# Two weight units staged in device memory, and another order of norms and transposes at two changes of stage

## Chip, cores, metric

One core of a Trainium2 chip runs the whole program; the other cores are idle. The metric is the device time of one execution in microseconds (us). Three executions of the kernel before took 946.19, 947.06 and 951.06 us, median 947.06.

## What is computed

The reference is a decoder trunk of two layers on 512 tokens of 1024 channels, all in float32. Layer 0 mixes tokens by trailing means over 2, 4, 8 and 16 tokens; layer 1 is attention over a window of 128 keys, with 16 query heads, 4 shared key and value heads and a sink logit per head. Each layer ends with a gated feed-forward part of width 2816 with a causal convolution of width 3. Every part has a norm ahead of it and one behind it:

```
for layer in range(2):
    h = rms_norm(x, mix_pre_g[layer])
    if layer == 0: m = pool_mixer(h, pool_w, pool_scale)
    else:          k, v = rms_norm(x, kv_norm_g) @ w_kv ; q = rope(h @ w_q)
                   m = attention(q, rope(k), v, sinks) @ w_o
    x = x + rms_norm(m, mix_post_g[layer])
    f = conv_glu_ffn(rms_norm(x, ffn_pre_g[layer]), w_in, conv_w, conv_b, w_out)
    x = x + rms_norm(f, ffn_post_g[layer])
```

## The kernel before

**Tiling.** The tokens are four blocks of 128 (b = 0 to 3), the channels eight chunks of 128. Every float32 product is made of three matmuls on reduced-precision parts: each operand is split into a high part (a copy that rounds, on ScalarE, `wh`, `xTh`, `gh`) and a low part (the difference, on VectorE, `wl`, `xTl`, `gl`), and `mm3` adds high x high, high x low and low x high in PSUM.

**Weights.** All large weights come as 95 numbered units of 128x2048, in the order of use. 1 to 22 are layer 0's up projection, 23 to 42 its down projection, 43 and 44 K and V, 45 to 48 Q, 49 to 52 the output projection, 53 to 74 layer 1's up projection, 75 to 94 its down projection. `load` brings a unit to a `raw` buffer (two of them) on SP's DMA queue, `split` makes its high and low part in one of three slots (two kinds of unit have a place of their own), and `ahead` splits three units ahead of use. Units 43 to 46 are made otherwise: `prepare` loads them half by half during layer 0's up projection, multiplies a norm's gain into them, splits them, and stores both parts in device memory (`ready`); later `split` only loads the finished parts into a slot, by DMAs that ScalarE issues. The first two units of an up projection, 53 and 54 in layer 1, are split in quarters by `low`, the low part on GpSimd.

**Order.** The order of the instructions on TensorE, VectorE, ScalarE and GpSimd is the order in which the code is written; each engine works through its own list and waits for others by semaphores. The order on SP's queue is set by the scheduler.

**Layer 0's second pass** (`pass2`). The down projection is done by a scheme with seven products on 2x2 blocks; the second pass has the last three. While TensorE goes through the pairs p = 0 to 10 for the products 3 and 2, the other engines prepare coming units (`soon(k)`: one unit's split, then the split of the matching G tile), and finish blocks 2 and 3 of the stream, which need only earlier products: `update(b)` adds to x, `pre_a(b)` takes the squares on ScalarE (`rstd_of`) and the inverse root on GpSimd in three 128x1 steps (an addition of epsilon, an addition of the two halves, a power), `pre_b(b)` scales x by it, `to_attention(b)` transposes the result on TensorE (tiles `tr_a`, L299) into `xTh_a` and `xTl_a`. Before, blocks 2's and 3's `pre_a` and `pre_b` stand together behind p = 1, and `to_attention` behind p = 5 and p = 6. In units: p = 4 and 5 need unit 39, p = 6 and 7 unit 40, p = 8 and 9 unit 41, p = 10 unit 42. The last three pairs are taken for block 0 and 2 first (i = 0), then for 1 and 3. Behind this pass come the K and V projections of blocks 2 and 3 (`kp`, `vp`), then `to_attention(0)`. `pass2` serves both layers; the calls under `then` are made in layer 0 only.

**End of attention.** The output projection is added up in all eight PSUM banks (`op`), first the products of one pair of heads, then those of the other. Block by block, `o_proj(1, b)` ends it with 24 matmuls; `post_norm` adds the normed result to x (squares on ScalarE, L247; root on GpSimd, L254 to L258; gain, L272, and update, L274, on VectorE), `pre_norm` makes the feed-forward part's input from it (the same squares and root, then L291), and `transpose_in` transposes it on TensorE (`tr_f`) and splits it (ScalarE L302, VectorE L303). Between these stand the quarters of units 53 and 54 (casts L189 on ScalarE, subtractions L193 on GpSimd). Then `start1` begins the up projection (`u`) with the units 53 and 54 on blocks 0 and 1; block 2's transposes follow behind the first of them.

Of the kernel before, what the change touches and what calls it, by code (L numbers as in the profile page):

```python
# [39 lines left out]
N_UNITS = 95  # L40
N_SLOTS = 3
# [29 lines left out]
def build(nc, tc, ctx, a, out):  # L71
# [44 lines left out]

    mhalf = pc.tile([P, 1], F32, tag="mhalf", name="mhalf")
# [11 lines left out]
    ready = {i: [dram(f"{n}{i}", 2048) for n in ("hi", "lo")] for i in (U_K, U_V, U_Q, U_Q + 1)}  # L129
# [29 lines left out]
    def prepare(i, h):  # L159
# [5 lines left out]
        for k in range(4):  # L165
# [77 lines left out]
    def rstd_of(src, junk, name):  # L243

        ss = pc.tile([P, 4], F32, tag="ss", name=f"ss_{name}", bufs=6)
        for h in range(2):
            nc.scalar.activation(junk[h], src[h], AF.Square, scale=1.0 / math.sqrt(D),  # L247
                                 accum_out=ss[:, h : h + 1])
            if h == 0:
                add_eps(ss, 0)  # L250
        return rstd_end(ss)

    def add_eps(ss, h):
        nc.gpsimd.tensor_scalar(ss[:, h : h + 1], ss[:, h : h + 1], EPS, None, ALU.add)  # L254

    def rstd_end(ss):
        nc.gpsimd.tensor_tensor(ss[:, 2:3], ss[:, 0:1], ss[:, 1:2], ALU.add)
        nc.gpsimd.tensor_tensor(ss[:, 3:4], ss[:, 2:3], mhalf, ALU.pow)  # L258
        return ss[:, 3:4]

# [21 lines left out]
    def pre_b(b):  # L282
        for h in range(2):
            nc.scalar.activation(halves(xna[b])[h], halves(x[b])[h], AF.Identity, scale=xnr[b])
# [230 lines left out]
    def first(l, xT, accs, p1, G2):  # L515
# [54 lines left out]
        for j in range(NF):  # L570
# [7 lines left out]
            if l == 0 and 3 <= j < 11:  # L578
                prepare((U_K, U_V, U_Q, U_Q + 1)[(j - 3) // 2], (j - 3) % 2)
# [32 lines left out]
    def pass2(l, p2, G2, X, post_row):  # L612
# [52 lines left out]
        def square(z, i, q):  # L665

            b, h = i + (2 if z[0] == "2" else 0), int(z[1]) - 1
            first = b not in ss
            if first:
                ss[b] = pc.tile([P, 4], F32, tag="ss", name=f"ss_p_f{l}{b}", bufs=6)  # L670
            nc.scalar.activation(X[q][i], Z[z][i], AF.Square, scale=1.0 / math.sqrt(D), accum_out=ss[b][:, h : h + 1])  # L671
            if first:
                add_eps(ss[b], h)
# [20 lines left out]
        for m in range(3):  # L694
# [3 lines left out]
            if m < 2:  # L698
                nc.vector.tensor_tensor(Z["22"][m], Z["12"][m], X[7][m], ALU.add)
                add("21", m, 7)  # L700
                square("22", m, 7)
# [11 lines left out]
        for p in range(NP - NT):  # L713
            for q in of:
                make(q, p, (0, 1))
            if p == 0:
                for i in range(2):
                    add("21", i, 4)
                    square("21", i, 4)
                    root(2 + i)  # L720
                soon(5)
                for i in range(2):
                    gain("21", i)
                for i in range(2):
                    update(2 + i)
                soon(6)
            if p == 1:
                then(pre_a, 2)
                then(pre_a, 3)
                soon(7)  # L730
                then(pre_b, 2)
                then(pre_b, 3)
            if p == 5:
                then(to_attention, 2)
# [415 lines left out]
```

## Time and profile before

| | |
|---|---|
| median of three executions | 947.06 us |
| the profiled execution's own time | 945.61 us |
| its span, first to last instruction | 943.5 us |
| busy on TensorE / VectorE / ScalarE / GpSimd | 97% / 69% / 50% / 36% |
| mean granted TensorE clock | 0.988 |

A row of a timeline gives start and duration in us, engine, source line, operation, the tiles written and read, their shape, how many like instructions in a row are merged, and in brackets the idle time of the engine just before with what ended it. PE is TensorE, PEld its weight loads, DVE VectorE, ACT ScalarE, POOL GpSimd, SP the engine that issues most DMAs. Matmuls overlap, so their durations are longer than their distance. A row of the view by stretches gives the stretch, its length, busy us of each engine with the number of instructions, the granted clock, the DMA engines' busy share and GB/s. A row of DMA issues gives the number, the size of one, and the median us from issue to landing. Tile names in the profile lack their numbers: `wl` is the low part of any unit.

### The profile page before, as it was taken

Reading aid. Unit: us, or ns where it says so; the run is one execution under the profiler, and the core shown is the slowest. Engines: PE = TensorE matmul, PEld = TensorE weight load, DVE = VectorE, ACT = ScalarE, POOL = GpSimd, SP = SyncE. Lnnn points to the kernel's source line nnn. Section 1 sums busy time; section 2 is a strip of 40 time slices with the busy share of each in tenths; the row PEclk is TensorE's granted clock in tenths of the full one; section 3 lists DMA queues with packets and bytes.
Section 4 is the critical chain, followed back from the end, with each engine's and each line's share of the span. In section 5 each row is a group of like instructions: output and inputs, shape, how many; then the busy total and the mean of one; then the engine's idle time right before and its main releaser. Section 6 shows DMA issues by size and latency. Waiting matters only on the chain.

```text
span 943.5 us, 12767 instructions
## 1 busy us (share of the span) xinstructions
PE 911.8 (97%) x4702; PEld 781.1 (83%) x4702; DVE 654.3 (69%) x940; ACT 469.5 (50%) x823; POOL 337.9 (36%) x389
## 2 busy tenths in 40 slices
PE   9999999999999999899999996999999999999996
PEld 8888888888888877799899885988888888888784
DVE  5878888765567788545999747466555565677886
ACT  5645444533345566454788634433333433455562
POOL 3725444433341002325566226144444433410001
PEclk9999999999999999899999997999999999999998
DMA  8356899855555664740112214444555555456652
GB/s 304 123 192 222 324 332 319 296 198 189 190 177 149 217 211 147 278 162 19 45 46 91 90 45 149 142 179 179 187 206 198 197 204 191 160 164 196 222 186 87
DMA packets 43024, 170.10 MB, mean 180 GB/s; under 512 B 5073, under 2 KB 6609, under 8 KB 34898
## 3 DMA queue, kind: packets, MB, share of 16 engines
q1 hardware_dynamic: 41810, 160.90, 48.7%
q10 hardware_dynamic: 1152, 8.39, 2.3%
q8 instruction: 37, 0.61, 0.3%
q14 instruction: 25, 0.20, 0.1%
HBM read 135.72 MB, written 33.55 MB: 179 GB/s over the span
## 4 chain that ended last, share of the span: by engine, by line
PE 76%; DVE 11%; DMA 3%; issue 3%; ACT 3%; POOL 3%; SPq 0%; POOLq 0%; DVEq 0%; ACTq 0%
PE u L307 17%; PE u L308 17%; PE u L306 17%; PE dn L306 4%; PE dn L307 4%; PE dn L308 4%; DVE xn_f L291 2%; DVE wl L227 2%; DVE P L895 1%; DMA raw<-in_ws_dram 1%; DVE x L274 1%; DMA raw<-t 1%; PE op L306 1%; PE op L307 1%; PE op L308 1%
## 5 line engine op out<-in xcount | busy, mean ns | idle before, releaser
L306 PE MATMUL u<-xTh_f,wh 128*128 128x512 f32 (+1 forms) x768 | 286.7, 373 | 4.5 <-ACT xTh_f L302 4.5
L307 PE MATMUL u<-xTl_f,wh 128*128 128x512 f32 (+1 forms) x768 | 286.2, 373 | 4.3 <-DVE xTl_f L303 4.3
L308 PE MATMUL u<-xTh_f,wl 128*128 128x512 f32 (+1 forms) x768 | 286.0, 372 | 0.0
L227 DVE TENSOR_TENSOR wl<-raw,wh 128x1024 fp32r<-128x1024 f32 (+1 forms) x158 | 204.6, 1335 | 14.2 <-ACT wh L226 13.9
L306 PEld LDWEIGHTS u<-xTh_f,wh 128*128 128x128 f32 x768 | 145.6, 190 | 30.1 <-ACT xTh_f L302 5.0
L307 PEld LDWEIGHTS u<-xTl_f,wh 128*128 128x128 f32 x768 | 145.5, 189 | 29.4 <-DVE xTl_f L303 4.8
L524 DVE SCALAR_TENSOR_TENSOR t<-u,conv,t 128x511 f32<-128x511 f32 x88 | 65.8, 748 | 148.0 <-ACT t L523 148.0
L308 PEld LDWEIGHTS u<-xTh_f,wl 128*128 128x128 f32 x768 | 145.5, 189 | 24.9
L226 ACT CAST wh<-raw 128x1024 fp32r<-128x1024 f32 (+1 forms) x158 | 156.8, 1041 | 12.7 <-DMA raw<-t 6.9
L523 ACT ACTIVATE t<-u,conv 128x512 f32<-128x512 f32 x88 | 68.2, 777 | 137.9 <-PE u L308 100.8
L544 POOL TENSOR_TENSOR G<-G,G 128x256 f32<-128x256 f32 x22 | 33.3, 1515 | 278.1 <-DVE G L539 278.1
L307 PE MATMUL dn<-wl,gh 128*128 128x512 f32 x276 | 108.1, 392 | 1.4 <-DVE wl L227 1.4
L308 PE MATMUL dn<-wh,gl 128*128 128x512 f32 x276 | 108.0, 391 | 1.2 <-DVE gl L637 1.2
L306 PE MATMUL dn<-wh,gh 128*128 128x512 f32 x276 | 108.1, 392 | 0.0
L532 ACT ACTIVATE t<-t 128x512 f32<-128x512 f32 x44 | 27.8, 632 | 104.6 <-DVE t L525 104.6
L525 DVE SCALAR_TENSOR_TENSOR t<-u,conv,t 128x510 f32<-128x510 f32 x88 | 65.9, 749 | 3.1
L307 PEld LDWEIGHTS dn<-wl,gh 128*128 128x128 f32 x276 | 52.1, 189 | 13.0 <-DVE wl L227 2.3
L254 POOL TENSOR_SCALAR ss_p_f<-ss_p_f 128x1 f32<-128x1 f32 x8 | 2.8, 354 | 166.6 <-ACT dn L671 166.6
L308 PEld LDWEIGHTS dn<-wh,gl 128*128 128x128 f32 x276 | 52.1, 189 | 12.4 <-DVE gl L637 1.6
L306 PEld LDWEIGHTS dn<-wh,gh 128*128 128x128 f32 x276 | 52.2, 189 | 10.8
L565 ACT CAST gh<-G 128x1024 fp32r<-128x1024 f32 x22 | 23.1, 1052 | 55.3 <-DVE G L563 40.8
L566 DVE TENSOR_TENSOR gl<-G,gh 128x1024 fp32r<-128x1024 f32 x22 | 28.0, 1274 | 26.6 <-ACT gh L565 21.1
(194 smaller groups left out, 1555.0 us busy)
## 6 DMA issues: line engine op xcount, KB each, us to landing
raw<-in_ws_dram SPq DMA_DIRECT2D x51, 1024.0 KB, 4.9
q<-in_ws_dram SPq DMA_DIRECT2D x44, 512.0 KB, 5.8
raw<-t SPq DMA_DIRECT2D x24, 768.0 KB, 5.5
t<-q SPq DMA_DIRECT2D x44, 256.0 KB, 2.9
t<-q SPq DMA_DIRECT2D x22, 512.0 KB, 2.7
raw<-in_ws_dram SPq DMA_DIRECT2D x22, 512.0 KB, 4.4
raw<-in_ws_dram SPq DMA_DIRECT2D x22, 256.0 KB, 3.9
r<-in_ws_dram SPq DMA_DIRECT2D x8, 512.0 KB, 7.0
```

The source lines that it names most:

```text
L226: nc.scalar.copy(hi[:, s], r[:, s])
L227: nc.vector.tensor_tensor(lo[:, s], r[:, s], hi[:, s].bitcast(F32), ALU.subtract)
L306: nc.tensor.matmul(acc, ah, bh, start=first, stop=False)
L307: nc.tensor.matmul(acc, ah, bl, start=False, stop=False)
L308: nc.tensor.matmul(acc, al, bh, start=False, stop=last)
L523: nc.scalar.activation(t, u, AF.Identity, bias=conv_col(l, ch, 3), scale=conv_col(l, ch, 2))
L524: nc.vector.scalar_tensor_tensor(t[:, 1:], u[:, : S - 1], conv_col(l, ch, 1), t[:, 1:], ALU.mult, ALU.add)
L525: nc.vector.scalar_tensor_tensor(t[:, 2:], u[:, : S - 2], conv_col(l, ch, 0), t[:, 2:], ALU.mult, ALU.add)
L532: nc.scalar.activation(tg, tg, AF.Gelu_apprx_tanh)
L544: nc.gpsimd.tensor_tensor(s1, s1, G2[:, p, 2, :], ALU.add)
L565: nc.scalar.copy(h, G1[:, o : o + 1024])
L566: nc.vector.tensor_tensor(lo, G1[:, o : o + 1024], h.bitcast(F32), ALU.subtract)
```

## The change

1. Units 53 and 54 join the units that `prepare` stages in device memory (`READY`). No gain belongs to them, so a half is one cast on ScalarE and one subtraction on VectorE. The twelve halves are no longer made in steps j = 3 to 10 of layer 0's up projection, one a step, but in two of every three steps from 3 to 19. At the end of attention eight ScalarE casts and eight GpSimd subtractions go, and four DMAs of 1 MB, issued by ScalarE, come: one pair ahead of block 0's `o_proj`, one ahead of block 1's. SP loads raw units 55 and 56 where 53 and 54 were loaded.
2. In `pass2`, in both layers, `soon(6)` goes ahead of the updates of blocks 2 and 3. In layer 0, `pre_a` and `pre_b` of block 2 come behind p = 2, then `soon(7)`, then block 3's; `pre_b` of these two blocks goes from ScalarE to VectorE; block 2's transposes go behind p = 7, block 3's behind the product 3 of the last three pairs for i = 0; V's loads go ahead of them, and block 1's last square and root ahead of block 0's norm.
3. At the end of attention `o_proj(1, 3)` is cut into its two halves, with block 1's transposes between them; block 0's transposes stand where they stood. On ScalarE and VectorE the split of the transposed block 0 now stands ahead of block 2's post-norm, that of block 1 ahead of block 3's; before, each stood between that block's post-norm and its pre-norm.
4. The instruction that preloads the Exp table reads `nsink` instead of a constant. The rest renames functions.

```
+READY = (U_K, U_V, U_Q, U_Q + 1, U_IN[1], U_IN[1] + 1)
...
-        for k in range(4):
+        if i >= U_IN[1]:
+            nc.scalar.copy(hi, r)
+            nc.vector.tensor_tensor(r.bitcast(F32R), r, hi.bitcast(F32), ALU.subtract)
+        for k in range(4 if i < U_IN[1] else 0):
...
     def pre_b(b):
         for h in range(2):
-            nc.scalar.activation(halves(xna[b])[h], halves(x[b])[h], AF.Identity, scale=xnr[b])
+            o, i = halves(xna[b])[h], halves(x[b])[h]
+            if b < 2:
+                nc.scalar.activation(o, i, AF.Identity, scale=xnr[b])
+            else:
+                nc.vector.tensor_scalar(o, i, xnr[b], None, ALU.mult)
...
-            if l == 0 and 3 <= j < 11:
-                prepare((U_K, U_V, U_Q, U_Q + 1)[(j - 3) // 2], (j - 3) % 2)
+            if l == 0 and j >= 3 and j % 3 != 2 and j < 21:
+                k = (j - 3) // 3 * 2 + j % 3
+                prepare(READY[k // 2], k % 2)
...
                 soon(5)
                 for i in range(2):
                     gain("21", i)
+                soon(6)
                 for i in range(2):
                     update(2 + i)
-                soon(6)
-            if p == 1:
+            if p == 2:
                 then(pre_a, 2)
+                then(pre_b, 2)
+                soon(7)
                 then(pre_a, 3)
-                soon(7)
-                then(pre_b, 2)
                 then(pre_b, 3)
             if p == 5:
-                then(to_attention, 2)
                 soon(8)
                 then(split, U_K)
-            if p == 6:
-                then(to_attention, 3)
+            if p == 7:
+                then(split, U_V)
+                then(to_attention, 2)
 
         for i in range(2):
             for q in of:
                 for p in range(NP - NT, NP):
                     make(q, p, (i,))
-        then(split, U_V)
+                if i == 0 and q == 3:
+                    then(to_attention, 3)
...
-        nc.scalar.activation(tab, mhalf, AF.Exp)
+        nc.scalar.activation(tab, nsink[:, 0:1], AF.Exp)
...
-        u0, u1 = U_IN[1], U_IN[1] + 1
         for b in range(NB):
-            u = (u0, u1)[b // 2]
-            o_proj(1, b, os[1, b])
+            if b < 2:
+                split(U_IN[1] + b)
+            o_proj(1, b, os[1, b], (0,))
+            if b == 3:
+                transpose_in(1, xnf[1], xT, "f1")
+            o_proj(1, b, os[1, b], (1,))
+            if b == 2:
+                transpose_in(0, xnf[0], xT, "f1")
             post_norm(b, acc[b], post_row, "m1", pa)
-            low(u, b % 2 * 2)
-            if b > 1:
-                transpose_in(b - 2, xnf[b - 2], xT, "f1")
             xnf[b] = pre_norm(b, pre_row, "f1")
-            low(u, b % 2 * 2 + 1)
```

The first place is VectorE's list in layer 0's second pass, before. Z2 is blocks 2 and 3 of the down projection; `wl40` is unit 40's low part, `gl3_0_3` that of the G tile used with it; `ss_n_a2` holds block 2's inverse root.

```order
L676 TENSOR_TENSOR Z2_0_2774<-Z2_0_2774,fpost0_724 128x512 x2
L685 SCALAR_TENSOR_TENSOR x2_75<-Z2_0_2774,ss_p_f02_2850,x2_75 128x512 x2
L685 SCALAR_TENSOR_TENSOR x3_76<-Z2_0_2774,ss_p_f03_2892,x3_76 128x512 x2
L227 TENSOR_TENSOR wl40_2968<-raw40_2919,wh40_2967 128x1024 x2
L637 TENSOR_TENSOR gl3_0_3_2976<-G2_0_729,gh3_0_3_2975 128x1024
L227 TENSOR_TENSOR wl41_3006<-raw41_2954,wh41_3005 128x1024 x2
L637 TENSOR_TENSOR gl3_0_4_3012<-G2_0_729,gh3_0_4_3011 128x1024
L303 TENSOR_TENSOR xTl_a_3068<-tr_a20_3069,xTh_a_3067 128x512
```

And the same piece in the changed kernel:

```order
L687 TENSOR_TENSOR Z2_0_2806<-Z2_0_2806,fpost0_728 128x512 x2
L232 TENSOR_TENSOR wl40_2996<-raw40_2951,wh40_2995 128x1024 x2
L650 TENSOR_TENSOR gl3_0_3_3004<-G2_0_733,gh3_0_3_3003 128x1024
L696 SCALAR_TENSOR_TENSOR x2_75<-Z2_0_2806,ss_p_f02_2882,x2_75 128x512 x2
L696 SCALAR_TENSOR_TENSOR x3_76<-Z2_0_2806,ss_p_f03_2924,x3_76 128x512 x2
L296 TENSOR_SCALAR xn_a2_3035<-x2_75,ss_n_a2_3036 128x512 x2
L232 TENSOR_TENSOR wl41_3045<-raw41_2986,wh41_3044 128x1024 x2
L650 TENSOR_TENSOR gl3_0_4_3051<-G2_0_733,gh3_0_4_3050 128x1024
L296 TENSOR_SCALAR xn_a3_3054<-x3_76,ss_n_a3_3055 128x512 x2
L232 TENSOR_TENSOR wl42_3100<-raw42_3001,wh42_3099 128x1024
L650 TENSOR_TENSOR gl3_0_5_3104<-G2_0_733,gh3_0_5_3103 128x512
```

Unit 40 with its G tile went ahead of the updates, and the two normalisations, each waiting for a root, now stand on VectorE between the units 40, 41 and 42.

The second place is ScalarE's list at the end of attention, before, from block 0's squares on (`pt_m10` is block 0's post-norm, `xn_f10` its pre-norm):

```order
L247 ACTIVATE pt_m10_1_5265,ss_p_m10_5266<-op01_4936 128x512
L189 CAST wh53_5276<-raw53_4950 128x512
L247 ACTIVATE xn_f10_5280,ss_n_f10_5281<-x0_73 128x512 x2
L189 CAST wh53_5276<-raw53_4950 128x512
L247 ACTIVATE pt_m11_0_5315,ss_p_m11_5317<-op10_5013 128x512
L247 ACTIVATE pt_m11_1_5316,ss_p_m11_5317<-op11_5076 128x512
```

And in the changed kernel, from just ahead of it:

```order
L966 CAST PTho3_5264<-o32_13_5041 128x512
L214 DMA wh53_5268<-hi53_121 128x2048
L214 DMA wl53_5269<-lo53_122 128x2048
L250 ACTIVATE pt_m10_0_5298,ss_p_m10_5300<-op00_4955 128x512
L250 ACTIVATE pt_m10_1_5299,ss_p_m10_5300<-op01_4968 128x512
L250 ACTIVATE xn_f10_5310,ss_n_f10_5311<-x0_73 128x512 x2
L214 DMA wh54_5319<-hi54_123 128x2048
L214 DMA wl54_5320<-lo54_124 128x2048
L250 ACTIVATE pt_m11_0_5349,ss_p_m11_5351<-op10_5043 128x512
```

The casts between the squares are gone, and four DMA issues stand in the list, the first pair ahead of block 0's squares.

The third place is SP's queue at the end of layer 1's second pass, before (`raw94` is the last unit's load, the others are stores of the output):

```order
L152 DMA raw93_7831<-in_ws_dram 128x1024 x2
L687 DMA out_0_dram<-x2_75 128x512 x2
L687 DMA out_0_dram<-x3_76 128x512 x2
L152 DMA raw94_7854<-in_ws_dram 128x1024
L687 DMA out_0_dram<-x0_73 128x512 x2
```

And in the changed kernel:

```order
L154 DMA raw93_7847<-in_ws_dram 128x1024 x2
L154 DMA raw94_7862<-in_ws_dram 128x1024
L698 DMA out_0_dram<-x2_75 128x512 x2
L698 DMA out_0_dram<-x3_76 128x512 x2
L698 DMA out_0_dram<-x0_73 128x512 x2
```

The last unit's load went ahead of the four stores of blocks 2 and 3.

More of the change, by code (lines that the diff above doesn't have):

```diff
@@ L127, in build @@
     sums4 = [[dram(f"t4_{l}_{m}", 2048) for m in range(3)] for l in range(2)]
-    ready = {i: [dram(f"{n}{i}", 2048) for n in ("hi", "lo")] for i in (U_K, U_V, U_Q, U_Q + 1)}
+    ready = {i: [dram(f"{n}{i}", 2048) for n in ("hi", "lo")] for i in READY}
     def source(i):
@@ L240, in bcast_row, with square, new_ss @@
         return t
[L243 to L254, printed above, removed]
+    def square(junk, src, ss, h, first):
+        nc.scalar.activation(junk, src, AF.Square, scale=1.0 / math.sqrt(D), accum_out=ss[:, h : h + 1])
+        if first:
+            nc.gpsimd.tensor_scalar(ss[:, h : h + 1], ss[:, h : h + 1], EPS, None, ALU.add)
+    def new_ss(name):
+        return pc.tile([P, 4], F32, tag="ss", name=f"ss_{name}", bufs=6)
     def rstd_end(ss):
@@ L259, in rstd_end, with rstd_of @@
         return ss[:, 3:4]
+    def rstd_of(src, junk, name):
+        ss = new_ss(name)
+        for h in range(2):
+            square(junk[h], src[h], ss, h, h == 0)
+        return rstd_end(ss)
     def halves(t):
@@ L663, in pass2, with square_of @@
         ss, rs = {}, {}
-        def square(z, i, q):
-            b, h = i + (2 if z[0] == "2" else 0), int(z[1]) - 1
+        def square_of(z, i, q):
+            b = i + (2 if z[0] == "2" else 0)
             first = b not in ss
             if first:
[L670 to L673, printed above, removed]
+                ss[b] = new_ss(f"p_f{l}{b}")
+            square(X[q][i], Z[z][i], ss[b], int(z[1]) - 1, first)
         def gain(z, i):
@@ L700, in pass2 @@
                 add("21", m, 7)
-                square("22", m, 7)
+                square_of("22", m, 7)
             else:
@@ L718, in pass2 @@
                     add("21", i, 4)
-                    square("21", i, 4)
+                    square_of("21", i, 4)
                     root(2 + i)
@@ L743, in pass2 @@
                     make(q, p, (i,))
-        then(split, U_V)
+                if i == 0 and q == 3:
+                    then(to_attention, 3)
         add("12", 0, 3)
-        square("12", 0, 3)
+        square_of("12", 0, 3)
         add("11", 0, 2)
-        square("11", 0, 2)
+        square_of("11", 0, 2)
         root(0)
@@ L752, in pass2 @@
         add("12", 1, 3)
-        square("12", 1, 3)
+        square_of("12", 1, 3)
         update(0)
-        then(pre_a, 0)
         add("11", 1, 2)
-        square("11", 1, 2)
+        square_of("11", 1, 2)
         root(1)
@@ L760, in pass2 @@
         gain("11", 1)
+        then(pre_a, 0)
+        update(1)
         then(pre_b, 0)
-        update(1)
         then(pre_a, 1)
```

## The prediction

> **What bounds the kernel now.** I read the page first, then TensorE's timeline for its idle stretches, then the timelines of the other engines around each of them.
>
> ```profile
> PE 911.8 (97%) x4702; PEld 781.1 (83%) x4702; DVE 654.3 (69%) x940; ACT 469.5 (50%) x823; POOL 337.9 (36%) x389
> ```
>
> TensorE sets the time. The change removes no matrix work, so all it can win is time in which TensorE stands still (943.5 - 911.8 = 31.7 us) or runs at a lower clock. On TensorE's timeline three places matter here. The first is the end of layer 0's second pass, just ahead of the K projection (kp).
>
> ```profile
> 371.74 0.39 PE L306 MATMUL dn<-wh,gh 128*128 128x512 f32 x1
> ...
> 374.91 0.39 PE L308 MATMUL dn<-wh,gl 128*128 128x512 f32 x1
> 381.44 1.97 PE L299 MATMUL tr_a<-cst,xn_a 128*128 128x128 f32 x8 [6.15 <-ACT xn_a L284]
> ...
> 387.18 1.03 PE L299 MATMUL tr_a<-cst,xn_a 128*128 128x128 f32 x8
> ...
> 398.95 0.28 PE L306 MATMUL kp<-wh,xTh_a 128*128 128x256 f32 x1
> ```
>
> TensorE waits 6.15 us for the normalised block 2. The second is the end of attention, where layer 1's first up units begin (573.51 is block 1's transposes, 590.74 block 2's), shown with the same start in layer 0 (38.47 to 44.41), which runs without a wait:
>
> ```profile
> 573.51 1.03 PE L299 MATMUL tr_f<-cst,xn_f 128*128 128x128 f32 x8
> 578.81 0.58 PE L306 MATMUL u<-xTh_f,wh 128*128 128x256 f32 x1 [4.27 <-ACT xTh_f L302]
> 583.31 0.58 PE L307 MATMUL u<-xTl_f,wh 128*128 128x256 f32 x1 [3.92 <-DVE xTl_f L303]
> ...
> 590.74 1.04 PE L299 MATMUL tr_f<-cst,xn_f 128*128 128x128 f32 x8
> ...
> 38.47 0.47 PE L306 MATMUL u<-xTh_f,wh 128*128 128x256 f32 x1
> ...
> 44.41 1.03 PE L299 MATMUL tr_f<-cst,xn_f 128*128 128x128 f32 x8
> ```
>
> Behind both stops the granted clock (the last figure but two) is half:
>
> ```profile
> 381.44:385.80 4.36, 4.36 (x15) 3.78 (x16) 1.93 (x3) 4.20 (x7) 0.41 (x1) 0.50 0.60 209
> ...
> 583.31:587.20 3.89, 3.89 (x18) 3.89 (x19) 2.97 (x3) 0.62 (x3) 2.00 (x3) 0.50 0.93 334
> ```
>
> The third is a short stop in layer 1's second pass:
>
> ```profile
> 922.37 0.50 PE L308 MATMUL dn<-wh,gl 128*128 128x512 f32 x1 [1.16 <-DVE gl L637]
> ```
>
> **Place 1, the change in layer 0's second pass.** What held TensorE up is on GpSimd and VectorE:
>
> ```profile
> 372.71 7.29 POOL L257 TENSOR_TENSOR ss_n_a<-ss_n_a 128x1 f32<-128x1 f32 x1 [0.16 <-ACT xn_a L247]
> 380.07 0.57 POOL L258 TENSOR_TENSOR ss_n_a<-ss_n_a,mhalf 128x1 f32<-128x1 f32 x1
> ...
> 370.40 2.73 DVE L685 SCALAR_TENSOR_TENSOR x<-Z,ss_p_f,x 128x512 f32<-128x512 f32 x4
> 373.05 2.35 DVE L227 TENSOR_TENSOR wl<-raw,wh 128x1024 fp32r<-128x1024 f32 x2
> 375.32 1.21 DVE L637 TENSOR_TENSOR gl<-G,gh 128x1024 fp32r<-128x1024 f32 x1
> ...
> 378.72 1.21 DVE L637 TENSOR_TENSOR gl<-G,gh 128x1024 fp32r<-128x1024 f32 x1
> ...
> 386.30 0.68 DVE L637 TENSOR_TENSOR gl<-G,gh 128x512 fp32r<-128x512 f32 x1
> ...
> 15.63 0.88 DVE L341 TENSOR_SCALAR xm<-x,ss_m 128x512 f32<-128x512 f32 x2 [0.27 <-POOL ss_m L258]
> ...
> 371.18 0.63 ACT L247 ACTIVATE xn_a<-x 128x512 f32<-128x512 f32 x1 [0.68 <-DVE x L685]
> ...
> 373.79 1.98 ACT L226 CAST wh<-raw 128x1024 fp32r<-128x1024 f32 x2
> 375.68 1.04 ACT L636 CAST gh<-G 128x1024 fp32r<-128x1024 f32 x1
> ```
>
> An add of 128x1 took 7.29 us: it ends at 380.00, when VectorE's six splits in a row end (378.72 + 1.21 = 379.93). In the new order VectorE stops by itself ahead of each normalisation, waiting for that root, so GpSimd gets through. [...]
>
> New times, keeping everything ahead of 370.40. VectorE: split 40 with its G parts takes 375.32 + 1.13 - 373.05 = 3.40 (a split alone is (378.72 - 373.05) / 5 = 1.13), to 373.80; the four updates 2.65, to 376.45. ScalarE's squares of block 2 start 0.78 behind the update's start (371.18 - 370.40), at 374.58, and take 2.61 / 2 = 1.31. GpSimd ends the root by 376.5 + 0.2 + 0.7 = 377.3 even if shut out during the updates. Normalisation 0.88: 378.2. Split 41 and its parts: 381.6. Block 3's squares lie behind ScalarE's casts of 41 (375.9 + 1.89 + 1.04 = 378.8) and are done at 380.2; its root, shut out until 381.6, ends at 382.6; normalisation 383.5; split 42 (1.13) 384.6; its parts (0.68) 385.3.
>
> TensorE: a matmul takes (374.91 - 371.74) / 14 = 0.226 us, and eight transposes 0.9 (398.95 - 387.18 less 48 matmuls). The transposes now stand behind two more products (24 matmuls): 375.14 + 5.43 = 380.57, block 2 long ready. Then 0.9 and 6 matmuls to 382.83, and there it needs split 42 and its parts: 385.3 instead of 383.3. Behind that 28 matmuls and the other transposes, 7.2, so kp starts at **392.5**. Before it was 398.95: **6.4 us won**, with about 2 us of waiting left. Best end: no wait at all, 375.14 + 60 x 0.226 + 1.8 = 390.5, 8.4 won. Worst: 2 us later and the clock halved again for some 4 us, 2.2 won.
>
> The later reordering there (block 1's last square ahead of block 0's norm) delays block 0's by one square, 0.6; its transposes come only behind four projections of K and V, 11.9 us at 5.94 a pair, so nothing. The same holds for the table preload, which now waits for an early GpSimd step.
>
> **Place 2, the end of attention.** A chain per block runs squares, root, update of x, squares, root, normalisation, and GpSimd's weight splits (L193) lie in it:
>
> ```profile
> 556.46 0.60 ACT L247 ACTIVATE pt_m<-op 128x512 f32<-128x512 f32 x1 [2.03 <-PE op L308]
> ...
> 558.10 1.29 POOL L193 TENSOR_TENSOR wl<-raw,wh 128x512 fp32r<-128x512 f32 x1
> ...
> 558.16 2.43 DVE L274 SCALAR_TENSOR_TENSOR x<-pt_m,ss_p_m,x 128x512 f32<-128x512 f32 x2 [0.30 <-POOL ss_p_m L258]
> ...
> 559.97 0.63 ACT L247 ACTIVATE xn_f<-x 128x512 f32<-128x512 f32 x1 [2.31 <-DVE x L274]
> ...
> 562.36 2.44 DVE L291 SCALAR_TENSOR_TENSOR xn_f<-x,ss_n_f,fpre 128x512 f32<-128x512 f32 x2 [1.77 <-POOL ss_n_f L258]
> ...
> 564.72 1.28 DVE L272 TENSOR_TENSOR pt_m<-op,mpost 128x512 f32<-128x512 f32 x2
> ...
> 591.38 1.08 ACT L302 CAST xTh_f<-tr_f 128x512 fp32r<-128x512 f32 x2 [7.45 <-PE tr_f L299]
> ...
> 592.00 1.29 DVE L303 TENSOR_TENSOR xTl_f<-tr_f,xTh_f 128x512 fp32r<-128x512 f32 x2 [5.14 <-ACT xTh_f L302]
> ```
>
> The pair of L274 takes 2.43 beside the GpSimd split of 558.10, where four of the same kind (L685) take 2.73, or 1.4 a pair. Without those splits, and with the eight ScalarE casts (L189) gone, the links are: second square to update 1.70 (558.16 - 556.46), update to squares 0.78, squares to normalisation 2.39 (562.36 - 559.97), normalisation 1.4. Block 0: update 558.16, squares 558.94, normalised 562.7. Block 1: second square 24 matmuls (5.43) later than block 0's, 561.9; gains 562.7 to 564.0 on VectorE, update 564.0, squares 564.8, normalised 568.5. Block 0's transposes stand where they stood, 573.51 - 24 x 0.226 - 0.9 = 567.2; casts 567.8 to 568.9, low parts 568.5 to 569.8. Block 2: second square 569.5, update 571.2, squares 572.0, normalised 575.7. Block 1's transposes now come half a projection earlier: 567.2 + 0.9 + 12 x 0.226 = 570.8; ScalarE casts them behind block 2's squares, 573.3 to 574.4; VectorE's low parts come behind block 2's normalisation, first half ready at 576.4. TensorE ends the projection's other half at 574.4 and waits for that, 1.8 us. The remaining 47 matmuls at 5.94 / 48 bring block 2's transposes to **582.2**, not 590.74: **8.5 won**. Best: no wait, 574.4 + 5.94 = 580.35, 10.4 won. Worst: the low part 2 us later and half clock for 4 us, 4.5 won.
>
> What the change adds is covered. Units 53 and 54 come by four loads of 1 MB on ScalarE's queue. The first pair waits there for unit 49's slot, until the last product of the first head pair, 556.46 - 0.2 - 24 x 0.226 = 550.8; queued behind it are block 0's squares, which wait for later matmuls anyway. The second pair goes behind block 0's second squares, at about 560. Use is at 574 and 583, 14 us and more behind the last issue of each. Their preparation in layer 0 is four steps with one cast (1.04) and one split (1.21) each. VectorE is busy 127 of 180 us there and TensorE never waits:
>
> ```profile
> 100.00:280.00 180.00, 180.00 (x795) 149.04 (x795) 126.82 (x148) 80.59 (x115) 75.79 (x57) 1.00 0.72 255
> ...
> 231.76 2.35 DVE L227 TENSOR_TENSOR wl<-raw,wh 128x1024 fp32r<-128x1024 f32 x2
> ...
> 239.65 0.78 ACT L523 ACTIVATE t<-u,conv 128x512 f32<-128x512 f32 x1 [2.37 <-PE u L308]
> ```
>
> The split of 231.76 is ready at 234.1, and TensorE comes to a new unit at 239.6: 5.5 us spare, of which 1.2 go. Cost nothing; if the cover is gone, some us per step (a rival).
>
> **Place 3, layer 1.** The same swap puts split 92 and its parts ahead of four updates (2.65 us), so the part TensorE waited 1.16 us for is there, and unit 94's load leaves ahead of the output's.
>
> ```profile
> 924.50 1.22 DVE L637 TENSOR_TENSOR gl<-G,gh 128x1024 fp32r<-128x1024 f32 x1
> ```
>
> Next late would be this part; TensorE needs it 24 matmuls on, at 926.6, and it ends at 925.7. So **1.2 won**; ends 0 and 1.2.
>
> **Sum.** 6.4 + 8.5 + 1.2 = 16.1 us off the profiled execution, 945.61 (span 943.5 and 2.1 around it): 929.5. The median of the three runs shown is 947.06, 1.45 above it, so I forecast **931.0**.
>
> On the clock: 1.16 us of idling cost none, 3.92 and more came with half clock; my 2.0 and 1.8 lie between, nearer the first, and I take full clock. [...]
>
> **Rivals.** *The root is late again at place 1*: waiting grows by 2 us, the clock halves; 2.2 + 8.5 + 1.2 = 11.9, 935.2. For it: 7.29 us for one add. Against: VectorE now waits for it. Chance 0.10. *Place 2's chain is longer*: five engines' hand-overs in it; 6.4 + 4.5 + 1.2 = 12.1, 935.0. Chance 0.10; both, 939.2, 0.02.
>
> *The time goes into K and V.* Their four loads now leave together from 380.6, beside the raw loads.
>
> ```profile
> wl<-lo ACTq DMA_DIRECT2D x4, 1024.0 KB, 7.4
> ```
>
> At 7.4 us a pair K is there at 388.0 and V at 395.4, needed at 392.5 and 398.4. If sharing doubles both, K lands at 395.4, V at 410.2 with its use then at 401.3: 2.9 + 8.9 = 11.8 lost, 16.1 falls to 4.3, 942.8: no change. [...] Against: 7.4 was already measured beside raw loads. Chance 0.05.
>
> *Slower: staging in layer 0.* Loads and stores of the preparation stand in SP's one queue ahead of raw units. If a raw unit slips a whole step (48 matmuls, 10.9) at each of the four new steps, TensorE stops 4 x (10.9 - 5.5) = 21.6: 952.5. It decides from about 5.5 us of slip. Against: eight such steps cost no stop before. Chance 0.03.
>
> **Numbers.** The forecast has 0.70 (927 to 934). 0.5%, 4.7 us, is about what a measurement can tell from no change. Faster: 0.70 + 0.10 + 0.10 + 0.02 = 0.92; same 0.05; slower 0.03. Low end: all best ends, 8.4 + 10.4 + 1.2 = 20.0, against the profiled level: 925.5. High end: one of the first two rivals with place 3 lost and a us for V: 937.
>
> **To see it.** Right if TensorE waits about 2 us at split 42's parts (gl) and kp starts 6 us earlier; if GpSimd's adds of ss_n_a end within a us of VectorE's waits; if no half clock is left between 370 and 600; if L193's splits of 53 and 54 are gone and the first xTl_f wait is under 3 us; if the gl stop of layer 1 is gone. Wrong if a wait on a load (wh, wl or raw) stands in their place, or a stop in layer 0's up projection.

## The result and the profile after

The changed kernel took 933.09 us (median of four executions, 930.12 to 935.51) beside 946.74 us for the kernel before on the same chip: a ratio of 0.9845, 95% interval 0.9803 to 0.9886. The forecast was 931.0 us with a range of 925.5 to 937.0. The profiled execution of the changed kernel took 935.51 us, its span is 933.7 us, 9.8 us shorter than before's. Three executions that took far longer than the rest are left out of all comparisons: one of e7's five (1303.89 us at a mean granted clock of 0.653) and two of the kernel before beside e5 to e8 (1533.73 us at 0.556, and 4889.31 us).

The page, busy time of the engines in the changed kernel:

```profile
PE 912.5 (98%) x4702; PEld 781.0 (84%) x4702; DVE 654.2 (70%) x948; ACT 466.7 (50%) x815; POOL 324.0 (35%) x381
```

TensorE's matmuls are as many as before, and it is busy for 0.7 us longer, so by this count the whole gain is idle time gone (31.7 us before, 21.2 after). The half clock that left the two changed places does not show in the sum, since 10.24 us of it came at the start of this run. GpSimd lost 13.9 us, most of it the eight splits of units 53 and 54 (8 x 1.29 = 10.3). TensorE's timeline at the start, at layer 0's down projection and second pass, and at the end of attention:

```profile
11.68 0.77 PE L387 MATMUL pd<-band,xm 128*128 128x128 f32 x2 [2.31 <-DVE xm L353]
...
300.77 0.50 PE L319 MATMUL dn<-wl,gh 128*128 128x512 f32 x1 [0.35 <-DVE wl L232]
...
387.39 1.03 PE L311 MATMUL tr_a<-cst,xn_a 128*128 128x128 f32 x8
391.38 0.50 PE L319 MATMUL dn<-wl,gh 128*128 128x512 f32 x1 [1.32 <-DVE wl L232]
392.33 1.03 PE L311 MATMUL tr_a<-cst,xn_a 128*128 128x128 f32 x8
399.35 0.28 PE L318 MATMUL kp<-wh,xTh_a 128*128 128x256 f32 x1
...
571.17 1.03 PE L311 MATMUL tr_f<-cst,xn_f 128*128 128x128 f32 x8
576.67 0.39 PE L319 MATMUL u<-xTl_f,wh 128*128 128x256 f32 x1 [1.62 <-DVE xTl_f L315]
582.41 1.04 PE L311 MATMUL tr_f<-cst,xn_f 128*128 128x128 f32 x8
```

The 6.15 us wait for xn_a is gone, and what is left is the forecast wait at unit 42's split (1.32). The waits of 4.27 and 3.92 are gone, and the forecast one for xTl_f is left (1.62). The stop of 1.16 for gl in layer 1 is gone without a successor. At the start, where the diff changes nothing, a wait of 0.90 us (10.63 in before) is now 2.31, and a stop of 0.35 at the first products of the down projection is new.

The same kernel by stretches; the last figure but two is the granted clock:

```profile
11.74:21.98 10.24, 10.24 (x40) 9.59 (x41) 4.84 (x13) 3.73 (x10) 1.94 (x6) 0.50 0.95 378
375.00:400.00 25.00, 23.58 (x114) 19.17 (x113) 22.85 (x32) 13.70 (x26) 6.81 (x10) 1.00 0.80 313
570.00:600.00 30.00, 27.80 (x213) 26.33 (x212) 16.48 (x25) 12.80 (x27) 8.94 (x16) 1.00 0.41 140
```

At both changed places the clock is full now. In this run the half clock stands at the start instead, right behind the 2.31 us.

**Counted from a common point.** Since the start differs from run to run, distances are counted from block 0's first transposes (tr_f, 25.64 in before, 31.64 in after) to kp, from there to block 2's transposes in layer 1, and from there to the end of the span. The start, the first up projection and the first pass are split off by the first wait of the second pass (the 0.71 for wl, at 334.39 in before and 341.22 in after).

| us | before | after | difference |
|---|---|---|---|
| start to the first tr_f | 25.64 | 31.64 | +6.00 |
| to the first wait of the second pass | 308.75 | 309.58 | +0.83 |
| from there to kp | 64.56 | 58.13 | -6.43 |
| kp to block 2's tr_f | 191.79 | 183.06 | -8.73 |
| from there to the end | 352.76 | 351.29 | -1.47 |
| span | 943.5 | 933.7 | -9.8 |

### The profile page after: what moved, and what is told of

The parts are those of the page before. It is cut to its first block, busy times and chain, and to the rows that moved or that the text cites. A ratio compares the mean times of both kernels' runs of the same rounds, so it can differ in the third digit from the quotient of the medians.

```text
span 933.7 us, 12782 instructions
## 1 busy us (share of the span) xinstructions
PE 912.5 (98%) x4702; PEld 781.0 (84%) x4702; DVE 654.2 (70%) x948; ACT 466.7 (50%) x815; POOL 324.0 (35%) x381
## 4 chain that ended last, share of the span: by engine, by line
PE 79%; DVE 10%; issue 3%; POOL 3%; ACT 3%; DMA 2%; POOLq 0%; SPq 0%; DVEq 0%; ACTq 0%
PE u L319 16%; PE u L320 16%; PE u L318 16%; PE dn L319 5%; PE dn L320 5%; PE dn L318 5%; DVE wl L232 2%; DVE xn_f L303 1%; DVE P L907 1%; PE op L318 1%; PE op L319 1%; PE op L320 1%; PE qp L320 1%; PE qp L318 1%; PE qp L319 1%
```

## The experiments

Each was timed beside the kernel before on the same chip; ratios are to those runs. The distances are those of the table: first tr_f to kp (373.31 before, 367.71 after), kp to block 2's tr_f (191.79, 183.06), and the rest (352.76, 351.29).

### Each place alone

**Layer 0's second pass alone (e1).** The changed kernel with four staged units, before's end of attention, and layer 1's second pass as before:

```
-READY = (U_K, U_V, U_Q, U_Q + 1, U_IN[1], U_IN[1] + 1)
+READY = (U_K, U_V, U_Q, U_Q + 1)
...
-                soon(6)
+                then(soon, 6)
                 for i in range(2):
                     update(2 + i)
+                if l == 1:
+                    soon(6)
...
```

> The kernel before with the change of layer 0's second pass alone; no staging, the old end of attention, layer 1 as before. Distances are counted from block 0's first transposes (tr_f), since the start of the program differs from run to run; before: 373.31 us to the first matmul of the K projection (kp), 191.79 from there to block 2's transposes in layer 1, 352.76 from there to the end. Theory (the places are independent and each won what the two traces show): 366.9 to kp (6.4 less), the two later distances within 0.3 of before, the time some 6 us under before's. Rival (a win here is partly given back at the next place, since loads then come closer): the second distance longer by 2 or more, the time under 4 us better.

Measured: 940.2 us, 0.9927 (0.9905 to 0.9949). Distances 368.76, 192.49, 352.45. The place wins by itself, but in this profile only 4.55 us where 6.4 was expected. TensorE's wait at unit 42, and the stretches around it:

```profile
384.86 0.51 PE L319 MATMUL dn<-wl,gh 128*128 128x512 f32 x1 [1.60 <-DVE wl L232]
```

```profile
382.85:386.26 3.41, 1.71 (x9) 0.91 (x8) 3.41 (x6) 0.00 (x0) 0.00 (x0) 1.00 1.00 423
386.26:389.67 3.41, 3.41 (x13) 2.83 (x12) 2.32 (x4) 1.62 (x3) 0.00 (x0) 0.50 1.03 432
389.67:393.08 3.41, 3.41 (x16) 2.79 (x15) 2.35 (x4) 1.00 (x4) 1.08 (x3) 1.00 1.02 430
```

The wait is 1.60 us instead of 1.32, and 3.41 us at half clock follow, with 13 matmuls in them, six of these transposes, where the next 3.41 us hold 16 matmuls of full size. So the forecast "full clock" for this wait held in the profile of after and not here. The second distance is longer by 0.70, outside the 0.3 expected but short of the rival's 2, and the rival's time did not come (6.9 us better, not under 4).

**The end of attention alone (e2).** The kernel before with the staging and the new order there (parts 1 and 3 of the change).

```
+READY = (U_K, U_V, U_Q, U_Q + 1, U_IN[1], U_IN[1] + 1)
...
-            o_proj(1, b, os[1, b])
+            if b < 2:
+                split(U_IN[1] + b)
+            o_proj(1, b, os[1, b], (0,))
+            if b == 3:
+                transpose_in(1, xnf[1], xT, "f1")
+            o_proj(1, b, os[1, b], (1,))
...
```

> The kernel before with the staging of units 53 and 54 and the new end of attention; both second passes as before. Theory: 8.7 us less from kp to block 2's transposes (191.8 to 183.1), and 0.8 more ahead of kp (373.3 to 374.1), the price of the staging steps in layer 0's up projection, with a stop of some 0.35 at the start of the down projection; the time some 8 us under before's. Rival 1 (the 0.8 belongs to something else in the second pass): the first distance stays at 373.3. Rival 2 (the end of attention profits from the earlier kp): the second distance shrinks by under 7.

Measured: 937.8 us, 0.9908 (0.9885 to 0.9931). Distances 374.26, 183.12, 352.51: 8.67 won behind kp, 0.95 lost ahead of it, with a stop of 0.34 at the down projection's first products. Both rivals fall: the price belongs to the staging, and the place doesn't need the earlier kp.

**The swap in layer 1 alone (e3).**

```
+                if l == 1:
+                    soon(6)
                 for i in range(2):
                     update(2 + i)
-                soon(6)
+                then(soon, 6)
```

> The kernel before with one line moved, in layer 1 alone: the split of unit 92 and of its part of G ahead of the updates of blocks 2 and 3. Theory: the stop of 1.16 us for gl goes, the distance from block 2's transposes to the end falls from 352.76 by 1.2 to 1.5, all else as before; the time within what a measurement can tell. Rival (the next part, wl or gl of unit 93 or 94, is then late): a stop of about 1 us some 24 to 48 matmuls later and no change of the distance.

Measured: 944.46 us, 0.9977 (0.9963 to 0.9991); distances 373.11, 191.73, 351.35. The stop is gone and none has come in its place: 1.41 us.

### What the end of attention is made of

**Staging alone (e4).** Units 53 and 54 staged and loaded, no `low` there, the transposes of blocks 0 and 1 at their old places.

```
...
         for b in range(NB):
             u = (u0, u1)[b // 2]
+            if b < 2:
+                split(U_IN[1] + b)
             o_proj(1, b, os[1, b])
             post_norm(b, acc[b], post_row, "m1", pa)
-            low(u, b % 2 * 2)
...
-            low(u, b % 2 * 2 + 1)
```

> The kernel before with units 53 and 54 staged in device memory and loaded at the end of attention, but the transposes of blocks 0 and 1 at their old places in all lists. Theory (the weight splits cost on three engines, but block 1's transposes and their low parts in the old order keep the rest): 4 to 6 us of the 8.7 from kp to block 2's transposes, with a wait for xTl of block 1 of 2 us or more left and perhaps half clock behind it. Rival 1 (the splits were all of it): 8 us or more. Rival 2 (the order was nearly all of it): under 2 us. In each case 0.8 us more ahead of kp.

**The order alone (e5).** The new order of part 3, with the quarters of units 53 and 54 still split there by `low`, one behind each post-norm and one behind each pre-norm.

```
-            o_proj(1, b, os[1, b])
+            o_proj(1, b, os[1, b], (0,))
+            if b == 3:
+                transpose_in(1, xnf[1], xT, "f1")
+            o_proj(1, b, os[1, b], (1,))
+            if b == 2:
+                transpose_in(0, xnf[0], xT, "f1")
             post_norm(b, acc[b], post_row, "m1", pa)
             low(u, b % 2 * 2)
-            if b > 1:
-                transpose_in(b - 2, xnf[b - 2], xT, "f1")
             xnf[b] = pre_norm(b, pre_row, "f1")
```

> The kernel before with the new order of transposes at the end of attention alone; units 53 and 54 are still split there, on ScalarE and GpSimd, two quarters a block. Staging alone gave 6.1 us of the 8.7 from kp to block 2's transposes. Theory (the two parts add up): 2.6 us less, 189.2 against 191.8, the waits ahead of the first u products still 3 us or more, since updates and gains still run beside GpSimd's splits. Rival 1 (either part alone reaches most of it, since the first to break the chain takes the half clock away): 6 us or more less. Rival 2 (without the staging the order does nothing, or harm, since a late normalisation now also holds the middle of a projection): within 1 us of before or longer.

Measured: e4 939.63 us, 0.9929 (0.9904 to 0.9954), kp to block 2 185.67: 6.12 won, just above the 4 to 6 expected; 374.55 to kp, 1.24 more than before where 0.8 was expected. e5 944.25 us, 0.9973 (0.9957 to 0.9990), 190.17: 1.62 won, less than the 2.6 expected. Together 7.74 of the 8.7, so the two add up but for 1 us. VectorE's update and normalisation of block 0 in after and in e5, with GpSimd's split beside them in e5:

```profile
558.54 1.41 DVE L282 SCALAR_TENSOR_TENSOR x<-pt_m,ss_p_m,x 128x512 f32<-128x512 f32 x2 [0.30 <-POOL ss_p_m L259]
561.72 1.42 DVE L303 SCALAR_TENSOR_TENSOR xn_f<-x,ss_n_f,fpre 128x512 f32<-128x512 f32 x2 [1.77 <-POOL ss_n_f L259]
```

```profile
558.80 2.43 DVE L274 SCALAR_TENSOR_TENSOR x<-pt_m,ss_p_m,x 128x512 f32<-128x512 f32 x2 [0.30 <-POOL ss_p_m L258]
562.99 2.44 DVE L291 SCALAR_TENSOR_TENSOR xn_f<-x,ss_n_f,fpre 128x512 f32<-128x512 f32 x2 [1.77 <-POOL ss_n_f L258]
...
558.73 1.29 POOL L193 TENSOR_TENSOR wl<-raw,wh 128x512 fp32r<-128x512 f32 x1
562.93 1.30 POOL L193 TENSOR_TENSOR wl<-raw,wh 128x512 fp32r<-128x512 f32 x1
```

A pair takes 1.0 us longer beside such a split, in two links of each block's chain. That is what staging takes away on VectorE. ScalarE's casts leave with it, and no run takes the two apart. What the order takes away is the last wait: TensorE's first u products in e4 (one row) and in e5 (two):

```profile
582.54 0.58 PE L311 MATMUL u<-xTl_f,wh 128*128 128x256 f32 x1 [2.18 <-DVE xTl_f L307]
```

```profile
578.32 0.39 PE L306 MATMUL u<-xTh_f,wh 128*128 128x256 f32 x1 [2.04 <-ACT xTh_f L302]
581.35 0.58 PE L307 MATMUL u<-xTl_f,wh 128*128 128x256 f32 x1 [2.64 <-DVE xTl_f L303]
```

Half clock follows in e4 and in e5: behind these rows the 128x256 matmuls start 0.21 us apart, up to 585.48 in e4 and 587.28 in e5, and 0.12 apart from there on. In before it lasts 10.24 us (576.97 to 587.21), and in e2 and after, whose wait is 1.63 and 1.62, they start 0.12 apart from the second one on.

### What held the root up

**A root with a one-input addition (e6).** The prediction said that the addition of 128x1 was shut out as long as VectorE ran splits. Whether its form matters was open.

```
-        nc.gpsimd.tensor_tensor(ss[:, 2:3], ss[:, 0:1], ss[:, 1:2], ALU.add)
+        nc.gpsimd.tensor_scalar(ss[:, 2:3], ss[:, 0:1], ss[:, 1:2], None, ALU.add)
```

> The kernel before with one instruction in each root written in another form: the addition of the two halves as a tensor_scalar with the second half as a per-partition scalar, so that it has one input of 128x1 instead of two. Theory (an instruction of GpSimd with two inputs is shut out as long as VectorE runs splits back to back, one with one input gets in at the next instruction boundary): the addition in layer 0's second pass takes under 1.5 us instead of 7.29, and the power behind it, which still has two inputs, is shut out in its place, some 6 us; kp as before. Rival 1 (any GpSimd instruction is shut out there): the addition still takes 6 us or more, the power 0.6. Rival 2 (it was no matter of the form but of one chance moment): neither takes over 2 us, and kp comes about 4 us earlier.

Measured: 950.11 us, 1.0026 (1.0011 to 1.0041). GpSimd's three steps of that root, and VectorE's row beside them:

```profile
376.10 7.36 POOL L257 TENSOR_SCALAR ss_n_a<-ss_n_a 128x1 f32<-128x1 f32 x1 [0.18 <-ACT xn_a L247]
383.55 0.57 POOL L258 TENSOR_TENSOR ss_n_a<-ss_n_a,mhalf 128x1 f32<-128x1 f32 x1
```

```profile
376.42 2.36 DVE L227 TENSOR_TENSOR wl<-raw,wh 128x1024 fp32r<-128x1024 f32 x2
...
382.10 1.22 DVE L637 TENSOR_TENSOR gl<-G,gh 128x1024 fp32r<-128x1024 f32 x1
```

7.36 us with one input, ending 0.14 behind the last split (382.10 + 1.22 = 383.32, 376.10 + 7.36 = 383.46). The theory of the two inputs falls; what rival 1 expected came, 7.36 for the addition and 0.57 for the power. The form costs 0.09 us more where nothing holds it up (0.28 for 0.19). In this profile kp comes 2.6 us later than in before: the mixer's norms keep TensorE waiting longer (0.83 and 1.05 us shortly after 50 us, 0.49 and 1.04 in before), and half clock follows there: behind the second wait the 128x256 matmuls start 0.21 us apart up to 55.53, and 0.12 apart from there on.

**The normalisations back on ScalarE (e9).**

```
-            if b < 2:
+            if b < NB:
                 nc.scalar.activation(o, i, AF.Identity, scale=xnr[b])
```

> The changed kernel with the normalisations of blocks 2 and 3 (pre_b) back on ScalarE, everything else as changed. Theory of the prediction (the root gets through because VectorE stops by itself ahead of each normalisation): without these stops the addition of ss_n_a is shut out again beside the splits of units 41 and 42, and kp comes 4 us or more later than the 367.7 us behind block 0's first transposes. Rival (any engine that waits for the root in list order will do: ScalarE holds the casts of the next unit back, and so VectorE stops all the same): the additions end within 1.5 us of their start, kp within 2 us of 367.7, or within 2 of 369.5 if the wait at unit 42 halves the clock as it did in two of three runs.

Measured: 936.19 us, 0.9883 (0.9862 to 0.9904); kp at 373.02, 5.3 later than in after. GpSimd's steps of block 3's root, ScalarE's first half of that normalisation, TensorE's waits:

```profile
383.18 1.00 POOL L252 TENSOR_SCALAR ss_n_a<-ss_n_a 128x1 f32<-128x1 f32 x1 [4.91 <-ACT xn_a L250]
384.26 0.19 POOL L258 TENSOR_TENSOR ss_n_a<-ss_n_a 128x1 f32<-128x1 f32 x1
```

```profile
385.12 0.72 ACT L294 ACTIVATE xn_a<-x,ss_n_a 128x512 f32<-128x512 f32 x1 [1.42 <-POOL ss_n_a L259]
```

```profile
384.16 0.50 PE L320 MATMUL dn<-wh,gl 128*128 128x512 f32 x1 [0.90 <-DVE gl L650]
387.97 0.80 PE L318 MATMUL dn<-wh,gh 128*128 128x512 f32 x1 [2.61 <-ACT gh L649]
```

Each side was half right. The root got through in 1.00 and 0.19 us, as the rival had it, since ScalarE's wait keeps back the cast of the next unit and so VectorE's splits. But kp came as late as the theory had it, for another reason: the same kept-back cast is what TensorE needs next (2.61 us for gh, then half clock: the 128x512 matmuls from 392.03 to 393.72 start 0.42 us apart, those from 393.96 on 0.23). So in this order the normalisation is better on VectorE: on ScalarE it holds up the cast that each split begins with.

### The start, and what is left

**Five filling matmuls at the start (e7 in the changed kernel, e8 in before).**

```
     mix_weights()
+    keep_busy(5)
     mix_norm(2)
```

> The changed kernel with five more idle-filling matmuls on TensorE between the pool weights' row and the second block's mixer, where the profiled run of after waited 2.30 us for the second x block and then ran 10.24 us at half clock. Theory (the 6 us lost at the start of that run is the chance landing of an input, turned into half clock, and no effect of the change): block 0's first transposes start at 25.5 to 27, the median falls to about 930, and the runs lie within 2 us of one another. Rival 1 (the spread of 930.1 to 935.5 comes from somewhere else): the spread stays above 4 us. Rival 2 (the half clock at the start belongs to the changed program): the first transposes still start near 31 in the profiled run.

> The kernel before with the same five matmuls. Theory: the lowest times as before's (944 to 946), the long ones of 950 and more gone, the median 945 to 946. Rival (the matmuls delay the second block's mixer): 0.5 to 1 us slower than before's lowest in every run.

Measured: e7 931.2 us (four executions, 929.83 to 932.47), 0.9825 (0.9804 to 0.9846), first tr_f at 26.24; e8 946.13 us, 0.9991 (0.9977 to 1.0004). The lowest time stays (930.12 without), and the spread is 2.6 us instead of 5.4, not under 2; with four executions each, and the intervals of the two ratios overlapping, this alone does not show that the matmuls took the long runs away. That the 6 us at the start of the profiled run of after are no part of the change, other profiles show: e1 and e9 have the changed kernel's start without the five matmuls, and their first tr_f comes at 25.70 and 25.74; e4 has the start of before, waits 1.47 us there, runs 6.83 us at half clock, and comes at 29.40. For before the median is unchanged within what is measured, the longest of its 12 runs 948.89 where 27 without the matmuls had 950.67. In the profiled run of e7 half clock remains twice, for 3.41 us each: from 26.41 on, in the thin work around the first transposes (TensorE is busy for 2.62 of the 3.42 us ahead of it), and behind the wait at unit 42. TensorE's wait there, and the stretches around it:

```profile
386.63 0.49 PE L319 MATMUL dn<-wl,gh 128*128 128x512 f32 x1 [1.43 <-DVE wl L232]
```

```profile
384.81:388.22 3.41, 1.87 (x11) 1.11 (x9) 3.41 (x6) 0.02 (x1) 0.00 (x0) 1.00 1.02 430
388.22:391.63 3.41, 3.41 (x12) 2.73 (x11) 2.12 (x4) 1.88 (x4) 0.01 (x1) 0.50 1.02 428
```

**Both waits taken away (e10).** On top of e7: unit 42's split ahead of block 3's normalisation, its transposes one product later; at the end of attention block 1's transposes with casts and low parts ahead of block 2's pre-norm.

```
                 then(pre_a, 3)
+                soon(8)
                 then(pre_b, 3)
             if p == 5:
-                soon(8)
...
-                if i == 0 and q == 3:
+                if i == 0 and q == 2:
...
-            o_proj(1, b, os[1, b], (0,))
-            if b == 3:
-                transpose_in(1, xnf[1], xT, "f1")
-            o_proj(1, b, os[1, b], (1,))
+            o_proj(1, b, os[1, b], (0, 1) if b < 3 else (1,))
...
             post_norm(b, acc[b], post_row, "m1", pa)
+            if b == 2:
+                o_proj(1, 3, os[1, 3], (0,))
+                transpose_in(1, xnf[1], xT, "f1")
             xnf[b] = pre_norm(b, pre_row, "f1")
```

> The changed kernel with the five start matmuls and with both waits that it has left taken on: in the second pass unit 42's split and its part of G go ahead of block 3's normalisation, whose transposes go behind the next product; at the end of attention the first half of block 3's projection, block 1's transposes and their casts and low parts go ahead of block 2's pre-norm. Theory (the waits of 1.3 to 1.6 us at unit 42 and of 1.62 for xTl are each one instruction's place in VectorE's list): both gone, kp 366.3 us behind block 0's first transposes, 181.4 from there to block 2's transposes, no half clock between 60 us and the end; about 3 us off, the median near 928. Rival 1 (something else is late right behind): waits of 1 us or more for xn_a3, gl or xn_f in the same places and under 1 us gained. Rival 2 (block 2's later normalisation then holds up the first u products): the second distance longer than 183.1.

**The staging steps early (e11).** On top of e10:

```
-            if l == 0 and j >= 3 and j % 3 != 2 and j < 21:
-                k = (j - 3) // 3 * 2 + j % 3
-                prepare(READY[k // 2], k % 2)
+            if l == 0 and 3 <= j < 15:
+                prepare(READY[(j - 3) // 2], (j - 3) % 2)
```

> The same as the run before it, with the twelve halves of the staged units made one in every step from 3 to 14 of layer 0's up projection instead of two in three steps from 3 to 19. Theory (the 0.83 to 0.95 us that staging costs ahead of kp come from the last of its steps, 18 and 19, which delay the first splits of the down projection; the stop of 0.34 us at its first products is part of it): that stop is gone, kp 0.5 to 0.9 us earlier than in the run before. Rival (the price lies in the steps themselves, a split and a cast each): kp as before it; or, crowded, later, with stops inside the up projection.

Measured: e10 928.24 us (927.17 to 928.67), 0.9795 (0.9774 to 0.9816); e11 927.06 us (926.67 to 928.51), 0.9787 (0.9766 to 0.9809). In e10 kp comes 366.06 behind the first tr_f and block 2 182.20 behind kp, and both waits are gone. The second distance is 0.8 longer than expected: two small waits that after does not have stand in the K stage, 0.25 for a copy of K (kst) and 0.23 for block 0's low part (xTl_a), and the rest stays open. GpSimd and VectorE at block 3's root in e10, and the whole stretch from 60 us to near the end:

```profile
380.63 3.86 POOL L252 TENSOR_SCALAR ss_n_a<-ss_n_a 128x1 f32<-128x1 f32 x1 [2.28 <-ACT xn_a L250]
```

```profile
383.72 0.69 DVE L651 TENSOR_TENSOR gl<-G,gh 128x512 fp32r<-128x512 f32 x1
385.43 0.89 DVE L296 TENSOR_SCALAR xn_a<-x,ss_n_a 128x512 f32<-128x512 f32 x2 [1.02 <-POOL ss_n_a L259]
```

```profile
60.00:900.00 840.00, 835.36 (x4243) 711.08 (x4242) 590.57 (x853) 425.41 (x725) 293.61 (x322) 1.00 0.55 193
```

The root is shut out here too, for 3.86 us until the last split ends (383.72 + 0.69 = 384.41, 380.63 + 3.86 = 384.49), and it costs nothing, since the transposes were moved behind it. TensorE idles 4.64 us in 840, at a granted clock of 1.00; over the run's span of 925.4 us the mean is 0.999, which by my estimate leaves room for 2.8 us at half clock (0.0015 x 925.4 / 0.5), less than the 3.41 that followed the waits in e1 and e7.

In e11 the first wait of the second pass comes 308.75 us behind the first tr_f (309.60 in e10, 308.75 in before), so the price of staging is gone whole, with the same twelve halves made; 0.34 of it is lost again ahead of kp (365.55 against 366.06), where no single wait shows it.

## Why the prediction was right, step by step

- **Place 1, 6.4 us:** 6.43 in the profiled run. The wait left at split 42 was 1.32 for wl and some 0.4 for gl right behind it (the next matmul starts 0.60 us later, at 391.98, instead of 0.23), 1.7 where 2 was forecast. The step under it that was too simple is "I take full clock" for such a wait: at this place 1.32 left the clock alone, 1.43 (e7) and 1.60 (e1) were each followed by 3.41 us at half clock, up to 1.7 us lost. Place 1 is worth 4.6 (e1) to 6.4 us, as the clock falls there or not; that the profiled run of after kept it was luck.
- **The mechanism of place 1:** the prediction let a root that starts beside splits end only behind them ("shut out until 381.6"). So it was in e6 (7.36) and e10 (3.86). In after a root's step did get in between two splits. GpSimd's three rows of block 3's root, and VectorE's beside them:

```profile
386.55 0.98 POOL L252 TENSOR_SCALAR ss_n_a<-ss_n_a 128x1 f32<-128x1 f32 x1 [2.28 <-ACT xn_a L250]
387.61 1.03 POOL L258 TENSOR_TENSOR ss_n_a<-ss_n_a 128x1 f32<-128x1 f32 x1
```

```profile
385.10 2.35 DVE L232 TENSOR_TENSOR wl<-raw,wh 128x1024 fp32r<-128x1024 f32 x2
387.37 1.22 DVE L650 TENSOR_TENSOR gl<-G,gh 128x1024 fp32r<-128x1024 f32 x1
389.31 0.88 DVE L296 TENSOR_SCALAR xn_a<-x,ss_n_a 128x512 f32<-128x512 f32 x2 [0.72 <-POOL ss_n_a L259]
```

The first step ends at 387.53, 0.08 behind a split (385.10 + 2.35), with the next one already started; the second only at 388.64, behind that one (388.59). So each step that was held up ended 0.05 to 0.14 us behind the end of a split: of the last in its row in before, in e6, in e10, in e1 (2.12 for the same first step, to 381.85, behind 381.77) and for the second step in after, of one inside the row for the first step in after. The prediction's 1 us for a root behind splits was enough because VectorE then waits for it. Why a step gets in behind one split and not behind another was not shown.
- **Place 2, 8.5 us:** 8.73, and 8.67 alone (e2). The wait for xTl_f is 1.62 where 1.8 was forecast, the clock full, as it was not behind e7's shorter wait of 1.43 at unit 42 (see the last section). The gain is the sum of two causes: the staging, which takes the splits of 53 and 54 out of the chains (6.1), and the order of the transposes (1.6), and 1 us that only both give.
- **Place 3, 1.2 us:** 1.47, and 1.41 alone (e3).
- **Staging at nothing:** wrong by 0.83 us. "5.5 us spare, of which 1.2 go" was read from the middle of the up projection, and there it held: counted from the first tr_f, TensorE in after stays level with before through the whole up projection and falls behind at the first two units of the down projection, by 0.2 and 0.6 us. VectorE begins the split that TensorE waits for there 267.86 us behind the first tr_f instead of 266.73. Before and after:

```profile
292.37 2.35 DVE L227 TENSOR_TENSOR wl<-raw,wh 128x1024 fp32r<-128x1024 f32 x2
```

```profile
299.50 2.35 DVE L232 TENSOR_TENSOR wl<-raw,wh 128x1024 fp32r<-128x1024 f32 x2
```

In e11, where the steps end at j = 14, that split begins at 266.74 again and the price is gone. Which of the steps from 15 to 19 cost it was not taken apart.
- **The level:** 6.43 + 8.73 + 1.47 - 0.83 = 15.8 us, where the sum forecast 16.1. That it came so close is in part luck: places 2 and 3 gave 0.5 more than forecast, and staging took 0.8. The profiled run lost 6.0 of the 15.8 at the start, so it took 935.51 where the sum gave 929.5. The median gained 13.7 (946.74 - 933.09). The 2.1 us between it and what the places are worth are probably the start and unit 42: only one of the four executions has a trace, but their times follow the clock, 930.12, 932.48, 933.69 and 935.51 us at mean granted clocks of 0.998, 0.996, 0.994 and 0.992.
- **The rivals:** TensorE waited for no load of K or V and for no raw unit in layer 0. The four loads of K and V did not leave together, as that rival had it: K's were issued at 383.72 and 384.10, V's at 387.64 and 387.99.

## What to carry to other kernels

A tiny step on GpSimd that others wait for should not start beside a row of VectorE splits (here an addition of 128x1 took 7.29 us beside six of them, and the next one, with VectorE idle, 0.19): either let VectorE wait for it in its own list, or move its consumer behind the row. Short stops of TensorE were worth removing here even at 1.5 us: 3.41 us at half clock, up to 1.7 us more, followed the 1.43 of e7 and the 1.60 of e1, and e10, without the two stops, took 927.17 to 928.67 us where e7 took 929.83 to 932.47. A cost that is "covered" must be checked at the last step of its row, where the cover ends, and not in the middle.

## What the runs showed that was not expected

**Half clock came for 3.41, 6.83 or 10.24 us, and not by the length of the stop alone.** The stretches at half clock that rows of these runs mark out (the ones behind the last matmuls aside) were 6.83 and 10.24 us long in before, 10.24 in after, 3.41 in e1, 3.41 twice in e7, and 6.83 at the start of e4. Their rows in before:

```profile
379.00:385.82 6.82, 4.38 (x15) 3.80 (x16) 2.89 (x4) 4.97 (x8) 2.52 (x5) 0.50 0.60 201
576.97:587.21 10.24, 4.48 (x19) 4.19 (x20) 9.18 (x10) 4.12 (x12) 6.45 (x10) 0.50 0.51 162
```

The prediction set its 2.0 and 1.8 us between a wait of 1.16 without half clock and one of 3.92 with it, nearer the first. In the runs waits of 1.43 (e7) and 1.60 us (e1) were followed by half clock, waits of 1.62 and 1.63 (after, e2) were not. The stretch with the 1.62 us in after, and the one behind it:

```profile
574.94:578.35 3.41, 1.79 (x15) 1.68 (x15) 3.41 (x7) 0.77 (x4) 0.99 (x3) 1.00 0.00 0
578.35:581.76 3.41, 3.41 (x31) 3.41 (x30) 1.63 (x4) 1.34 (x4) 0.96 (x3) 1.00 0.67 153
```

TensorE's busy time is no larger here than in e7's stretch with the 1.43 us (1.79 against 1.87; e1's with the 1.60 has 1.71). The matmuls are 15 here, 11 in e7 and 9 in e1, but of different shapes. What decides whether the clock falls was not shown, and no run was made to test it. At the start the profiled run of after was at half clock for 10.24 us, that of e4 for 6.83, and their first tr_f came at 31.64 and 29.40; in the other seven profiled runs without the five filling matmuls it came at 25.21 to 26.89, in the four with them (e7, e8, e10, e11) at 25.76 to 26.24.
